# Sample outputs of attention, GLA and SSD: fold matmuls replaced by transposes, with copies or a DVE sum behind them

## The chip, the cores and the metric

The kernel runs on one core of a Trainium2 chip. The metric is the device time of one execution in microseconds. Three runs of the kernel before gave 2531.6, 2530.73 and 2526.93 us, the median is 2530.73 us.

A core has a matrix engine (TensorE, PE in the profile; its weight loads are PEld), a vector engine (DVE), a scalar engine (ACT) and GpSimd (POOL), which work through queues of their own, in order, and wait for one another through semaphores. SyncE (SP) issues transfers, POOL does too. Data lie in SBUF (128 partitions); TensorE writes PSUM, which DVE and ACT read.

## The reference, cut to what matters

One step of a decoder layer for two groups of tokens with the same weights: a prompt of 256 tokens, and 8 samples of 4 tokens (32 columns). All of it is float32.

```
xn = _rmsnorm(x, p['norm_mix'])
z, xbc, dt_raw, q, k, v, r, g_lr, gate_a, gate_b = _split(xn @ p['w_in'], IN_SIZES)
...
y_ssd, ssd_state_new = _ssd_scan(xs_h, dt, A, Bm, Cm, ssd_state)       # 32 heads in 4 groups
y_ssd = y_ssd + p['ssd_D'][:, None] * xs_h
u = y_ssd * silu(z);  u = u * rsqrt(mean(u * u) + EPS) * p['ssd_norm']
branch_a = u @ p['w_ssd_out']
...
o, gla_state_new = _gla_scan(qh, kh, vh, glog, gla_state)              # 4 heads
o = o * rsqrt(mean(o * o) + EPS) * p['gla_norm'] * silu(r)
branch_b = o @ p['w_gla_out']
merged = sigmoid(gate_a) * branch_a + sigmoid(gate_b) * branch_b
h = x + merged @ p['w_mix_out']
h = h + _cross_attend(_rmsnorm(h, p['norm_cross']), mem_k, mem_v, p['w_cq'], p['w_co'])   # 4 heads
up = _rmsnorm(h, p['norm_ffn']) @ p['w_up'];  ...  h = h + (silu(gt) * a) @ p['w_down']
```

For a sample, the part of a scan's output that matters here is a product with the sample's own state or memory: in SSD `einsum('bign,bgrpn->bigrp', Cc, S)`, in GLA `einsum('bihk,bhkv->bihv', qe, S)`, in attention `einsum('bhlm,bmhd->blhd', pr, mem_v)`. To it SSD and GLA add the part from the four tokens of the same sample.

## The kernel before

**Layout.** Activations lie with channels on the partitions and the T = 288 tokens in the columns: columns 0 to 255 are the prompt, 256 to 287 the samples (SEQ = 256, NS = 32, NB = 8 samples of NL = 4 tokens). A projection (`proj_w`, L132) goes over blocks of 256 output channels. For each pair of weight tiles ACT casts the raw tile to a high part (L103) and DVE subtracts it for a low part (L105); TensorE then does three matmuls for each weight tile (L147, L148 high part with both parts of the activations, L151 low part). Raw weights have 3 buffers, high and low parts 5 each. SP issues the weight transfers (L114).

**Stages.** Memory keys and values (L315 to L319); then eight units, the four SSD groups and the four GLA heads. `weave` (L172) runs the scan of unit n as background between the projection steps of unit n + 1 and the output projection of unit n - 1: the first 16 steps are of unit n + 1, and then `project(n - 1)` runs. After the last unit, `project(7)` follows at once. Then gates, mix, four cross-attention heads (`attend`, woven between query projections; the last head is woven between the first steps of the output projection `wo`), and the feed-forward part. The program gives the order in which the work is written; a scheduler with a timeline of its own decides each engine's order from it, except for instructions held with `keep_in_program_order` and a stretch at the start.

**The sample outputs.** The states of the 8 samples differ, so each sample needs a product of its own. With b = 4q + j (q 0 or 1, j 0 to 3), the product of sample b is written to the 32 partitions from 32j: the stationary operand (`qdm`, `cdm`, `pms`) holds 32 columns of which only 4b to 4b + 3 are not zero (`diag`, L191). Row 32j + 4b + l of the PSUM tile (L1138, L864, L1526) so holds the output of sample b, token l, and the other rows of the block only take zeros. In block j lie the samples j and 4 + j.

The part inside the four tokens is added in two ways. In GLA one matmul over all samples (L1133) with the mask tile `atsl` (filled at L1073 by `stack_l`: ACT's L655 for all 128 partitions, DVE's L656 for the last 64) puts it into rows 0 to 31. In SSD the heads are in two sets and L866 writes one set into rows 0 to 31 and the other into rows 32 to 63, each with all 32 sample tokens; DVE adds both to `ys` (L905, L908).

Then the 128 x 512 tile (`ys`, `os_`) is turned to channels on partitions, and its four blocks of rows are added: four matmuls with the 128 x 128 slice as stationary and `fold4` as moving operand, a 128 x 32 matrix of four identity matrices on top of each other (L914, L1161, L1554). Their outputs go side by side into a PSUM tile of tag `mm` (3 buffers).

**What follows each.** SSD: `us` (the D term) plus the result (L915), times silu(z) (L916), squares (L922, L925) added up by DVE (L926), then `finish`: L937 adds the squares over partitions by a matmul with ones, ACT makes the scale (L219, L220), DVE multiplies (L942) and splits into high and low part (L184, L185), tile `un`. GLA: `evac` squares on ACT (L1042) and multiplies on DVE (L1043), adds squares (L1044, L1045), then the same `finish`. Attention: `split` writes high (ACT, L188) and low (DVE, L189) part into `co`, the operand of the output projection.

`conv_cache` (L598) turns the state of the convolution, copies it with ACT (L603) to a tile of tag `cst` (2 buffers), and SP sends it out (L608). POOL issues the loads of the states: L727 and L715 in SSD, L1036 in GLA.

Of the kernel before, what the change touches and what calls it, by code (L numbers as in the profile page):

```python
# [8 lines left out]
F32 = mybir.dt.float32  # L9
# [3 lines left out]
ALU = mybir.AluOpType  # L13
AX = mybir.AxisListType
PSUM = bass.MemoryType.PSUM

P = 128
D = 2048
KT = D // P
SEQ = 256  # L20
NB = 8
NL = 4
NS = NB * NL
T = SEQ + NS
# [18 lines left out]
def hybrid_step(ctx: ExitStack, tc: tile.TileContext, I: dict, O: list):  # L43
# [3 lines left out]
    V, S, G = nc.vector, nc.scalar, nc.gpsimd  # L47
    MM, TR = nc.tensor.matmul, nc.tensor.transpose
# [12 lines left out]
    def acc_tiles(n):  # L61

        turn[0] += 1
        return [ps.tile([P, 512], F32, tag=f"acc{turn[0] % 2}", bufs=2, name="acc") for _ in range(n)]

    def mm_tile():
        return ps.tile([P, 512], F32, tag="mm", bufs=3, name="mm")
# [5 lines left out]
    ident = const.tile([P, P], F32, name="ident")  # L73
# [6 lines left out]
    fold4 = const.tile([P, NS], F32, name="fold4")  # L80
# [106 lines left out]
    def split(hi, lo, src):  # L187
        S.copy(hi, src)  # L188
        V.tensor_tensor(lo, src, hi, ALU.subtract)  # L189
# [13 lines left out]
    def halves(alloc, name):  # L203

        ts = [alloc(f"{name}{i}") for i in range(2)]

        def at(k, n=None):
            t, o = ts[k // 8], k % 8
            if n is None:
                return t[:, o, :], t[:, 8 + o, :]  # L210
            return t[:, o:o + n, :], t[:, 8 + o:8 + o + n, :]
        return at
# [40 lines left out]
    ats = p1.tile([P, NS], F32, name="ats")  # L253
    atsl = p1.tile([P, P], F32R, name="atsl")
# [11 lines left out]
    with pool("p0") as p0:  # L266
# [194 lines left out]
        for c in range(4):  # L461
            q = slice(c * NS, (c + 1) * NS)
# [112 lines left out]
    pa = pa_cm.__enter__()  # L575
# [4 lines left out]
    def b2(name):  # L580
        return pa.tile([P, 512], F32, tag="b2", bufs=10, name=name)
# [64 lines left out]
    def stack_r(dst, src):  # L646

        S.copy(dst, src)
        for q in (1, 3):
            rows = slice(q * NS, (q + 1) * NS)  # L650
            V.tensor_tensor(dst[rows], src[rows], dst[rows], ALU.subtract)

    def stack_l(dst, src):

        S.copy(dst, src)  # L655
        V.tensor_tensor(dst[2 * NS:], src[2 * NS:], dst[2 * NS:], ALU.subtract)  # L656
# [36 lines left out]
    def ssd_scan(g, xsT, sz):  # L693
# [39 lines left out]
        a = mm_tile()  # L733
# [9 lines left out]
        a = mm_tile()  # L743
# [9 lines left out]
        for i in range(2):  # L753
            a = mm_tile()
# [14 lines left out]
        a = mm_tile()  # L769
# [4 lines left out]
        a = mm_tile()  # L774
# [11 lines left out]
        for u in range(3):  # L786
# [19 lines left out]
            if prev is not None:  # L806
                uu, pm, pea = prev
                a = mm_tile()
                for w in range(2):
                    o = w * SEQ  # L810
                    for s in range(3):
                        for e in range(2):
                            q = 2 * w + e
                            hs = slice((4 * uu + q) * 64, (4 * uu + q + 1) * 64)
                            rows = slice(64 * e, 64 * e + 64)
# [27 lines left out]
        a = mm_tile()  # L843
# [6 lines left out]
        yield  # L850
        wst = r2("wst")
        stack_l(wst, wxs)
        yield

# [15 lines left out]
        for q in range(NB // 2):  # L870
# [12 lines left out]
            for t2 in range(2):  # L883
# [3 lines left out]
                a = mm_tile()  # L887
# [16 lines left out]
        ys = b2("ys")  # L904
        V.tensor_tensor(heads(ys), heads(ysi[0]), hb(eas[:, h0:h0 + 8], P), ALU.mult)  # L905
        for r in range(2):
            q, c = slice(NS * r, NS * r + NS), slice(256 * r, 256 * r + 256)
            V.tensor_tensor(ys[q, c], ys[q, c], ysa[0][q, c], ALU.add)  # L908
        us = b2("us").rearrange("p (t l) -> p t l", l=P)[:, :, 0:NS]
        V.tensor_tensor(us, xsT[:, :, SEQ:T], dcol[:, 4 * g:4 * g + 4].unsqueeze(2).to_broadcast([P, 4, NS]), ALU.mult)  # L910
        yield
        a = mm_tile()
        for t in range(4):
            MM(a[:, t * NS:(t + 1) * NS], ys[:, t * P:(t + 1) * P], fold4, start=True, stop=True)  # L914
        V.tensor_tensor(us, us, a[:, 0:4 * NS].rearrange("p (t l) -> p t l", l=NS), ALU.add)  # L915
        V.tensor_tensor(sz[:, :, SEQ:T], us, sz[:, :, SEQ:T], ALU.mult)  # L916
        yield

# [110 lines left out]
    def gla_scan(h, eb, qe, ke, kd, kde, vT, sr):  # L1029
# [9 lines left out]
        def evac(a, t0, n):  # L1039
            av = a[:, 0:4 * n].rearrange("p (t l) -> p t l", l=n)  # L1040
            s4 = b2("s4").rearrange("p (t l) -> p t l", l=P)[:, :, 0:n]
            S.activation(s4, av, ACT.Square)  # L1042
            V.tensor_tensor(sr[:, :, t0:t0 + n], av, sr[:, :, t0:t0 + n], ALU.mult)  # L1043
            V.tensor_tensor(s4[:, 0:2], s4[:, 0:2], s4[:, 2:4], ALU.add)  # L1044
            V.tensor_tensor(sq[:, t0:t0 + n], s4[:, 0, :], s4[:, 1, :], ALU.add)  # L1045
# [6 lines left out]
        for i in range(2):  # L1052
            a = mm_tile()
# [7 lines left out]
        a = mm_tile()  # L1061
        for i, (t0, n) in enumerate(TOK):
            for k in range(2):
                MM(a[:, t0:t0 + n], ke[:, k, t0:t0 + n] if i < 2 else ker[:, k, :], qe[:, k, t0:t0 + n],
                   start=(k == 0), stop=(k == 1))
        for i in range(2):
            for k in range(2):
                MM(a[:, 288 + 64 * i:352 + 64 * i], kd[:, k, P * i:P * i + P], qe[:, k, P * i + 64:P * i + P],
                   start=(k == 0), stop=(k == 1))
        V.copy_predicated(att, gmask.unsqueeze(1).to_broadcast([P, 2, P]),  # L1070
                          a[:, 0:SEQ].rearrange("p (c n) -> p c n", n=P))
        V.copy_predicated(ats, smaski, a[:, SEQ:T])
        stack_l(atsl[:, 0:NS], ats)  # L1073
        S.copy(att[0:64, :, 64:P], a[0:64, 288:416].rearrange("p (c n) -> p c n", n=64))
        for i in range(2):
            for k in range(2):
# [4 lines left out]
        a = mm_tile()  # L1081
# [5 lines left out]
        a = mm_tile()  # L1087
# [5 lines left out]
        a = mm_tile()  # L1093
        for k in range(2):
            TR(a[:, k * P:(k + 1) * P], ksr[:, k, :], ident)
        kst = pa.tile([P, 256], F32R, tag="kst", bufs=1, name="kst")
        stack_l(kst, a[:, 0:256])
        for k in range(2):
            diag(qdm[:, k], qe[:, k, SEQ:T])
# [7 lines left out]
        for i in range(2):  # L1107
            sn = c4([P, 2, 512], "sn")
            for k in range(2):
                a = mm_tile()  # L1110
# [7 lines left out]
            for t in range(4):  # L1118
                MM(o[:, t * P:(t + 1) * P], vt[i][:, t * P:(t + 1) * P], att[:, i, :], start=True, stop=(i == 0))
                if i == 1:  # L1120
                    for k in range(2):
                        MM(o[:, t * P:(t + 1) * P], sprev[:, k, t * P:(t + 1) * P], qe[:, k, P:SEQ], start=False,
                           stop=(k == 1))
# [10 lines left out]
        for q in range(2):  # L1134
            for k in (1, 0):
                for j in (3, 2, 1, 0):
                    b = 4 * q + j
                    MM(osa[NS * j:NS * j + NS, :], qdm[:, k, b, :], sins[b][:, k, :], start=False,  # L1138
                       stop=(q == 1 and k == 0))
            yield  # L1140
            for b in range(4 * q, 4 * q + 4):
# [3 lines left out]
                for k in range(2):  # L1145
                    a = mm_tile()
# [9 lines left out]
        os_ = b2("os")  # L1156
        S.copy(os_, osa)
        yield
        a = mm_tile()
        for t in range(4):  # L1160
            MM(a[:, t * NS:(t + 1) * NS], os_[:, t * P:(t + 1) * P], fold4, start=True, stop=True)  # L1161
        evac(a, SEQ, NS)
        yield
        yield
        yield from finish(sr, sq, rg, False)
# [69 lines left out]
    for n in range(8):  # L1235
        kind, i = units[n]
        scan = (ssd_scan if kind == "s" else gla_scan)(i, *outs[n][0])
        nxt = start(n + 1) if n < 7 else gate(O_GA, gate_a, GH)
        if n == 5:
            mb = bigf("mb")  # L1240
        parts = [nxt, gate(O_GA, gate_early, 0, GH)] if n == 0 else [steps(nxt, 16), project(n - 1), nxt]
        weave(chain(*parts), scan, N_MAIN[n], N_BG[n])
# [120 lines left out]
    co = halves(bigr2, "co")  # L1363
# [49 lines left out]
    def transpose_half(kv, d2):  # L1413

        a = mm_tile()
        for d in range(2):
            for m in range(2):
                dd = 2 * d2 + d
                TR(a[:, d * 256 + m * P:d * 256 + (m + 1) * P], kv[:, m, dd * P:(dd + 1) * P], ident)
        return a.rearrange("p (d m) -> p d m", m=256)  # L1420
# [30 lines left out]
    def attend(hd):  # L1451
# [26 lines left out]
        for d2 in range(2):  # L1478
            a = transpose_half(kvp[:, 0], d2)
# [4 lines left out]
        for l in range(2):  # L1484
            a = mm_tile()
# [18 lines left out]
        a = mm_tile()  # L1504
        TR(a[:, 0:P], pr, ident)
        for m in range(2):
            f, g = pms[:, m].rearrange("p b t -> p (b t)"), a[:, m * 64:(m + 1) * 64]
# [3 lines left out]
        a = mm_tile()  # L1511
# [11 lines left out]
        for q in (1, 0):  # L1523
            for m in range(2):
                for j in (3, 2, 1, 0):
                    mm = MM(osa[NS * j:NS * j + NS, :], pms[:, m, 4 * q + j, :], vcs[4 * q + j][:, m, :],  # L1526
                            start=(q == 1 and m == 0), stop=(q == 0 and m == 1))
# [9 lines left out]
        for d in range(4):  # L1537
            a = mm_tile()
# [10 lines left out]
        os_ = px.tile([P, 512], F32, tag="os", bufs=1, name="os")  # L1549
        S.copy(os_, osa)  # L1550
        yield
        a = mm_tile()
        for d in range(4):
            MM(a[:, d * NS:(d + 1) * NS], os_[:, d * P:(d + 1) * P], fold4, start=True, stop=True)  # L1554
        split(*(x[:, :, SEQ:T] for x in co(4 * hd, 4)),
              a[:, 0:4 * NS].rearrange("p (d l) -> p d l", l=NS))
        yield

    def first_keys():
# [11 lines left out]
    for hd in range(4):  # L1571
        main = q_proj(hd + 1) if hd < 3 else chain(steps(wo[0], 6), steps(wo[1], 6))
        weave(main, attend(hd), 16 if hd < 3 else 12, 22 if hd else 18)
# [158 lines left out]
    rows = [(0, slice(0, P)), (P, slice(0, P)), (T - P, slice(P - NS, P))]  # L1732
# [19 lines left out]
    a = acc_tiles(1)[0]  # L1752
# [62 lines left out]
```

## Time and profile before

| what | value |
|---|---|
| median of three runs | 2530.73 us |
| the profiled execution, own time | 2530.86 us |
| its span, first to last instruction | 2529.1 us |
| granted TensorE clock, mean | 0.997 |
| raw weight tiles cast by ACT (L103), mean | 618 ns, 1464 of them |
| their low parts on DVE (L105), mean | 686 ns, 1464 of them |
| fold matmul records (L914, L1161, L1554) | 96, mean 265 ns |
| traffic to and from HBM | 205 GB/s over the span |

How to read it: the profile names each group by line, engine, operation, output and inputs. A matmul's duration runs from its start to its modelled end, so successive matmuls overlap and their durations add to more than the time they take. The starts in the timeline show the pace. "Idle before" names the engine whose work the instruction waited for. The chain that ended last goes back from the last instruction, each time to what released it.

### The profile page before, as it was taken

The numbers are of one execution on the slowest core, as the hardware profiler recorded it, in microseconds if no ns is written. First come the engines' busy times: TensorE is split into PE (matmuls) and PEld (weight loads), VectorE is DVE, ScalarE is ACT, GpSimd is POOL, SyncE is SP. The second block draws the span as 40 slices with busy tenths as digits, with TensorE's granted clock in tenths as the row PEclk, the third lists the DMA queues.
The fourth block names the chain that finished last, engine by engine and source line by source line (L and its number), as shares of the span: only waits on it lengthen the run. The fifth ranks groups of instructions, "written<-read, shape, count | busy, mean of one in ns | idle before, by whom it ended". The sixth has DMA issues, their size and how long they took to land.

```text
span 2529.1 us, 50509 instructions
## 1 busy us (share of the span) xinstructions
PE 2508.4 (99%) x18962; PEld 2418.5 (96%) x18962; DVE 1747.9 (69%) x3744; ACT 1342.7 (53%) x2724; POOL 392.2 (16%) x729
## 2 busy tenths in 40 slices
PE   9999999999999999999999999999999999999998
PEld 8889999998999999999999998999999999999998
DVE  6656777786867656667666577667777677675765
ACT  7655647655463645454454554555555455454545
POOL 3002133342300000000001022402111001020010
PEclk9999999999999999999999999999999999999999
DMA  8766587767868676767777699655555555555553
GB/s 268 220 218 196 169 252 206 229 197 209 236 188 271 184 241 185 242 202 265 205 223 249 199 327 322 211 164 173 169 173 170 170 172 172 167 172 171 169 170 130
DMA packets 442022, 521.96 MB, mean 206 GB/s; under 512 B 26876, under 2 KB 390236, under 8 KB 441712
## 3 DMA queue, kind: packets, MB, share of 16 engines
q1 hardware_dynamic: 407728, 422.34, 54.3%
q0 software_dynamic: 34016, 96.38, 12.0%
q8 instruction: 149, 2.44, 0.4%
q14 instruction: 97, 0.79, 0.1%
q10 hardware_dynamic: 32, 0.01, 0.0%
HBM read 473.13 MB, written 45.48 MB: 205 GB/s over the span
## 4 chain that ended last, share of the span: by engine, by line
PE 96%; DMA 2%; DVE 1%; POOL 1%; ACT 0%; issue 0%; DVEq 0%; ACTq 0%
PE acc L148 27%; PE acc L147 27%; PE acc L151 27%; PE acc L315 2%; PE acc L316 2%; PE acc L319 2%; DMA sqr<-in_state_ssd_dram 1%; PE la L1526 1%; PE la L1468 1%; PE mm L1147 1%; PE la L1138 1%; PE mm L1111 1%; POOL sqr L727 0%; DMA raw<-in_w_gla_out_dram 0%; DMA raw<-in_w_in_dram 0%
## 5 line engine op out<-in xcount | busy, mean ns | idle before, releaser
L103 ACT CAST whi<-raw 128x512 fp32r<-128x512 f32 x1464 | 895.1, 618 | 1016.0 <-PE acc L148 753.2
L105 DVE TENSOR_TENSOR wlo<-raw,whi 128x512 fp32r<-128x512 f32 x1464 | 994.4, 686 | 621.5 <-ACT whi L103 607.9
L147 PE MATMUL acc<-xn,whi 128*128 128x288 f32 (+1 forms) x1936 | 550.5, 299 | 0.0
L148 PE MATMUL acc<-xn,whi 128*128 128x288 f32 (+1 forms) x1936 | 542.3, 296 | 0.0
L151 PE MATMUL acc<-xn,wlo 128*128 128x288 f32 (+1 forms) x1936 | 414.1, 295 | 0.0
L148 PE MATMUL acc<-hf,whi 128*128 128x288 f32 x1408 | 393.2, 295 | 0.0
L147 PE MATMUL acc<-hf,whi 128*128 128x288 f32 x1408 | 389.0, 292 | 0.0
L147 PEld LDWEIGHTS acc<-xn,whi 128*128 128x128 f32 (+1 forms) x1936 | 364.7, 188 | 9.8 <-issue 8.1
L148 PEld LDWEIGHTS acc<-xn,whi 128*128 128x128 f32 (+1 forms) x1936 | 365.0, 189 | 6.8 <-issue 4.9
L151 PEld LDWEIGHTS acc<-xn,wlo 128*128 128x128 f32 (+1 forms) x1936 | 310.5, 188 | 1.3 <-issue 1.1
L151 PE MATMUL acc<-hf,wlo 128*128 128x288 f32 x1408 | 294.5, 290 | 0.0
L148 PEld LDWEIGHTS acc<-hf,whi 128*128 128x128 f32 x1408 | 264.5, 188 | 0.1
L147 PEld LDWEIGHTS acc<-hf,whi 128*128 128x128 f32 x1408 | 264.0, 188 | 0.1
L151 PEld LDWEIGHTS acc<-hf,wlo 128*128 128x128 f32 x1408 | 226.1, 188 | 0.0
L148 PE MATMUL acc<-pr,whi 128*128 128x288 f32 x704 | 196.5, 295 | 0.0
L147 PE MATMUL acc<-pr,whi 128*128 128x288 f32 x704 | 195.0, 293 | 0.0
L147 PE MATMUL acc<-un,whi 128*128 128x288 f32 x512 | 145.8, 300 | 2.2 <-ACT whi L103 1.1
L151 PE MATMUL acc<-pr,wlo 128*128 128x288 f32 x704 | 147.4, 290 | 0.0
L148 PE MATMUL acc<-un,whi 128*128 128x288 f32 x512 | 142.9, 295 | 0.0
L1639 POOL COPY fsp<-fst 128x16 f32<-128x16 f32 x88 | 36.6, 419 | 656.5 <-DVE av L1651 422.0
L148 PEld LDWEIGHTS acc<-pr,whi 128*128 128x128 f32 x704 | 132.3, 188 | 0.0
L147 PEld LDWEIGHTS acc<-pr,whi 128*128 128x128 f32 x704 | 132.0, 188 | 0.0
(512 smaller groups left out, 4286.4 us busy)
## 6 DMA issues: line engine op xcount, KB each, us to landing
raw<-in_w_in_dram SPq DMA_DIRECT2D x240, 512.0 KB
raw<-in_w_up_dram SPq DMA_DIRECT2D x176, 512.0 KB
raw<-in_w_down_dram SPq DMA_DIRECT2D x88, 512.0 KB
raw<-in_w_cv_dram SPq DMA_DIRECT2D x32, 512.0 KB
raw<-in_w_ssd_out_dram SPq DMA_DIRECT2D x32, 512.0 KB
sin<-in_state_gla_dram POOLq DMA_DIRECT2D x32, 512.0 KB, 5.8
out_dram<-sin SPq DMA_DIRECT2D x32, 512.0 KB
raw<-in_w_gla_out_dram SPq DMA_DIRECT2D x32, 512.0 KB
```

The lines of the kernel that those rows point to most:

```text
L103: S.copy(hi, raw)
L105: V.tensor_tensor(lo, raw, hi, ALU.subtract)
L147: MM(a, hi[:, k, cs], xh, start=(k0 + s0 + k == 0), stop=False)
L148: MM(a, hi[:, k, cs], xl, start=False, stop=False)
L151: MM(a, lo[:, k, cs], xh, start=False, stop=(k0 + s0 + k == nk - 1))
L315: MM(accs[m], mn_hi[:, kk, ms_], hi[:, 0, :], start=(kk == 0), stop=False)
L316: MM(accs[m], mn_lo[:, kk, ms_], hi[:, 0, :], start=False, stop=False)
L319: MM(accs[m], mn_hi[:, kk, ms_], lo[:, 0, :], start=False, stop=(kk == KT - 1))
L1111: MM(a, kt[:, i, k * P:(k + 1) * P], vt[i], start=True, stop=True)
L1138: MM(osa[NS * j:NS * j + NS, :], qdm[:, k, b, :], sins[b][:, k, :], start=False, stop=(q == 1 and k == 0))
L1147: MM(a, kb[:, k * P:(k + 1) * P], vst, start=True, stop=True)
L1639: G.tensor_copy(sp[:, :, 0:2], st.rearrange("p (b k) -> p b k", k=2))
```

## The change

The twelve groups of four fold matmuls (4 SSD, 4 GLA, 4 attention) become four transposes each. A transpose gives 128 columns in place of 32, one for each row of the tile.

- Attention and GLA: the columns 36j + 16q + l are picked, for which `own` builds the address pattern. In attention `split` is called once for q = 0 and once for q = 1. In GLA two ACT copies bring the columns together in a new SBUF tile `ot` of tag `cst`, and `evac` reads that.
- GLA also writes the mask `atsl` so that the part inside the samples comes out in the rows 36j + 16q + l: the copy on ACT and the subtraction on DVE have a pattern of 2 x 4 x 4 columns in place of 32 in a row.
- SSD: DVE sums the four blocks with a `tensor_reduce` over a strided view of the PSUM tile, into a new tile `yt` of tag `cst`, and adds that to `us`.

```
+    def own(a, q):
+        return bass.AP(a.tensor, a.offset + 16 * q, [list(a.ap[0]), [P, 4], [NS + NL, 4], [1, NL]])
...
 # ssd_scan
-            MM(a[:, t * NS:(t + 1) * NS], ys[:, t * P:(t + 1) * P], fold4, start=True, stop=True)
-        V.tensor_tensor(us, us, a[:, 0:4 * NS].rearrange("p (t l) -> p t l", l=NS), ALU.add)
+            TR(a[:, t * P:(t + 1) * P], ys[:, t * P:(t + 1) * P], ident)
+        yt = pa.tile([P, P], F32, tag="cst", bufs=2, name="yt").rearrange("p (t l) -> p t l", l=NS)
+        V.tensor_reduce(yt, a.rearrange("p (t j l) -> p t l j", j=4, l=NS), axis=AX.X, op=ALU.add)
+        V.tensor_tensor(us, us, yt, ALU.add)
...
 # gla_scan
-        stack_l(atsl[:, 0:NS], ats)
+        for rows, op in ((slice(0, P), None), (slice(2 * NS, P), ALU.subtract)):
+            f, g = atsl[rows], ats[rows].rearrange("p (q j l) -> p q j l", j=4, l=NL)
+            f = bass.AP(f.tensor, f.offset, [list(f.ap[0]), [16, 2], [NS + NL, 4], [1, NL]])
+            if op is None:
+                S.copy(f, g)
+            else:
+                V.tensor_tensor(f, g, f, op)
...
-            MM(a[:, t * NS:(t + 1) * NS], os_[:, t * P:(t + 1) * P], fold4, start=True, stop=True)
-        evac(a, SEQ, NS)
+            TR(a[:, t * P:(t + 1) * P], os_[:, t * P:(t + 1) * P], ident)
+        ot = pa.tile([P, P], F32, tag="cst", bufs=2, name="ot")
+        for q in range(2):
+            S.copy(ot.rearrange("p (t q j l) -> p q t j l", t=4, q=2, j=4)[:, q], own(a, q))
+        evac(ot, SEQ, NS)
...
 # attend
-            MM(a[:, d * NS:(d + 1) * NS], os_[:, d * P:(d + 1) * P], fold4, start=True, stop=True)
-        split(*(x[:, :, SEQ:T] for x in co(4 * hd, 4)),
-              a[:, 0:4 * NS].rearrange("p (d l) -> p d l", l=NS))
+            TR(a[:, d * P:(d + 1) * P], os_[:, d * P:(d + 1) * P], ident)
+        for q in range(2):
+            split(*(x[:, :, SEQ + 16 * q:SEQ + 16 * q + 16].rearrange("p d (j l) -> p d j l", l=NL) for x in co(4 * hd, 4)),
+                  own(a, q))
```

## The prediction

> **What bounds the kernel now.** I read the page first: busy times, then the chain that ended last.
>
> ```profile
> span 2529.1 us, 50509 instructions
> ...
> PE 2508.4 (99%) x18962; PEld 2418.5 (96%) x18962; DVE 1747.9 (69%) x3744; ACT 1342.7 (53%) x2724; POOL 392.2 (16%) x729
> ...
> PE 96%; DMA 2%; DVE 1%; POOL 1%; ACT 0%; issue 0%; DVEq 0%; ACTq 0%
> ```
>
> TensorE carries 96% of the chain, and its weight loads are busy for nearly as long as its matmuls. So TensorE time that is taken out should shorten the run one for one, except where TensorE then waits. DVE (69%) and ACT (53%) have room on average, which says nothing of single places. Where TensorE waits today the view of waits tells:
>
> ```profile
> PE mm L890 <- ACT cst L603: 5.5, 1, 5.5
> ...
> PE acc L147 <- ACT whi L103: 1.1, 1, 1.1
> ...
> PE mm L777 <- DVE wx L761: 0.5, 1, 0.5
> PE acc L147 <- ACT co L188: 0.4, 1, 0.4
> ```
>
> These are the waits of places that the change can reach, each a single one, 7.5 us together (5.5 + 1.1 + 0.5 + 0.4). The long one is not ACT's doing. The chain in order of time, read around that place, shows a weight tile that took 8.9 us to land after state tiles had been loading:
>
> ```profile
> 552.48 5.39 DMA sqr<-in_state_ssd_dram
> ...
> 559.04 4.31 DMA sqr<-in_state_ssd_dram
> ...
> 565.21 8.90 DMA raw<-in_w_in_dram
> ...
> 574.73 0.61 ACT whi L103
> 575.35 0.17 ACT cst L603
> ```
>
> ACT's copy L603 stood in its queue behind the cast of that weight tile, and L890 behind the copy. I come back to it among the rivals.
>
> **TensorE: 12 groups of four.** Each SSD head group, GLA head and attention head ends in four fold matmuls; each becomes four transposes. The view of groups by shape has both kinds, since the kernel transposes elsewhere:
>
> ```profile
> L1554 PE MATMUL mm<-fold,os 128*128 128x32 f32 x32 | 3.9, 265 | 0.0
> L914 PE MATMUL mm<-fold,ys 128*128 128x32 f32 x32 | 3.9, 265 | 0.0
> L1161 PE MATMUL mm<-fold,os 128*128 128x32 f32 x32 | 3.9, 265 | 0.0
> ...
> L845 PE MATMUL mm<-ident,xsr 128*128 128x128 f32 x16 | 2.4, 272 | 0.0
> ```
>
> L1161 stands in a loop of four in four heads, 16 calls, and has 32 records: a fold is done in two passes. L845 is also a loop of four in four groups, and has 16 records: a transpose is one pass. So eight passes become four. Durations overlap (265 ns each), so the price is taken from starts, in the timeline around one group of each kind:
>
> ```profile
> 375.21 0.97 PE L914 MATMUL mm<-fold,ys 128*128 128x32 f32 x8
> ...
> 376.01 0.38 PE L147 MATMUL acc<-xn,whi 128*128 128x288 f32 x1
> ...
> 544.20 0.60 PE L845 MATMUL mm<-ident,xsr 128*128 128x128 f32 x4
> ...
> 544.55 0.38 PE L147 MATMUL acc<-un,whi 128*128 128x288 f32 x1
> ```
>
> From the first fold to the next projection matmul 0.80 us pass (376.01 - 375.21), from the first transpose 0.35 (544.55 - 544.20). The saving is 0.45 us a group, though the output is four times as wide: the pass counts, not its 32 or 128 columns. Eleven groups give 4.95 us.
>
> [...]
>
> **The twelfth group** is the last attention head's. Nothing else stands between it and the output projection:
>
> ```profile
> 1602.90 0.97 PE L1554 MATMUL mm<-fold,os 128*128 128x32 f32 x8
> 1603.10 0.37 ACT L188 CAST co<-mm 128x256 fp32r<-128x256 f32 x1 [0.22 <-PE mm L1543]
> 1603.52 0.42 DVE L189 TENSOR_TENSOR co<-mm,co 128x256 fp32r<-128x256 f32 x1
> 1603.91 0.27 ACT L188 CAST co<-mm 128x128 fp32r<-128x128 f32 x1 [0.44 <-PE mm L1554]
> 1604.21 0.29 DVE L189 TENSOR_TENSOR co<-mm,co 128x128 fp32r<-128x128 f32 x1 [0.27 <-ACT co L188]
> 1604.23 0.79 PE L147 MATMUL acc<-co,whi 128*128 128x288 f32 x4 [0.35 <-ACT co L188]
> ```
>
> The transposes end at 1602.90 + 0.60 = 1603.50, when ACT has just finished its copy before (1603.47). Then come two casts of 128x64 instead of one of 128x128. No row has that shape on ACT from PSUM; the nearest are 192 ns for 128x32 and 269 for 128x128:
>
> ```profile
> L620 ACT COPY cv<-acc 128x32 f32<-128x32 f32 x24 | 4.6, 192 | 0.0
> ...
> L1042 ACT ACTIVATE s<-mm 128x128 f32<-128x128 f32 x4 | 1.1, 269 | 0.1
> ```
>
> I take 0.23, the middle. Both end about 1603.54 + 2 x 0.23 = 1604.00, or 1603.92 to 1604.08 at the two ends, against 1604.18 now. So TensorE restarts 0.18 us earlier (0.10 to 0.26) instead of 0.45. DVE's two low parts follow while the four L147 run (0.79 us), so they hold nothing. Sum over twelve: 4.95 + 0.18 = 5.1 us.
>
> **What DVE and ACT get.** In SSD one add from PSUM is replaced by a reduction over all 512 columns and an add of 128. The nearest reductions and the third SSD group's finish:
>
> ```profile
> L1385 DVE TENSOR_REDUCE mx<-mm 128x1 f32<-128x256 f32 x8 | 3.4, 425 | 3.7 <-PE mm L1491 3.6
> ...
> L1402 DVE TENSOR_REDUCE mx<-la 128x1 f32<-128x128 f32 x4 | 1.2, 290 | 6.5 <-PE la L1468 6.5
> ...
> 614.50 0.97 PE L914 MATMUL mm<-fold,ys 128*128 128x32 f32 x8
> ...
> 615.51 0.29 DVE L915 TENSOR_TENSOR us<-us,mm 128x128 f32<-128x128 f32 x1 [1.31 <-PE mm L914]
> 616.32 0.28 DVE L916 TENSOR_TENSOR sz<-us,sz 128x128 f32<-128x128 f32 x1
> ...
> 617.45 1.59 DVE L926 TENSOR_TENSOR sqa<-sqa,th 128x288 f32<-128x288 f32 x3 [0.85 <-ACT th L925]
> ...
> 620.13 0.41 PE L937 MATMUL mm<-sqa,ones 128*128 128x288 f32 x1
> ```
>
> From 128 to 256 columns a reduction grows by 0.135 us, so 512 come to 0.425 + 2 x 0.135 = 0.70. Bounds: 0.43, the 256-column row, and 1.40, twice the line, since the four addends lie 32 columns apart and no row shows such a reduction. With L915 (0.29) as the price of the add, the path to the scale grows by 0.70 + 0.29 - 0.29 = 0.70. This group is the tightest: its L937 keeps its place in TensorE's order, while in the other three it stands 8, 9 and 32 matmuls later. DVE's last sum ends at 617.45 + 1.59 = 619.04, so L937 has 1.09 us of slack; DVE starts 0.45 earlier and so does TensorE, which leaves 1.09 - 0.70 = 0.39. A weight's low part (L105) now stands between L916 and L926, and the idle 0.85 before L926 takes it. At 1.40 the slack is gone by 0.31 us: TensorE would wait so long in this group, and behind it the projections. I count nothing, with 0.3 as its upper end.
>
> In GLA two ACT copies come ahead of L1042. Only the last head is followed at once by its consumer:
>
> ```profile
> 1180.18 0.65 PE L937 MATMUL mm<-sqa,ones 128*128 128x288 f32 x2
> ...
> 1186.13 1.80 DVE L185 SCALAR_TENSOR_TENSOR un<-sr,rg,un 128x288 fp32r<-128x288 f32 x4
> ...
> 1189.35 0.29 PE L147 MATMUL acc<-un,whi 128*128 128x288 f32 x1
> ```
>
> The normalized output is done at 1187.93, used at 1189.35: 1.42 us of cover. The change puts L937 four projection matmuls later, 0.13 each (0.53), and brings the use forward by 0.45; 0.44 is left. Were the cover gone, each tenth would be paid in full. The two copies (0.46) lie within the 0.53. The mask's moved pieces hold as many elements as before, and their one reader, L1133, comes only after both chunk steps of the head. SP and POOL keep their order, so no DMA is added or moved past another. The new tile shares two buffers with the convolution-state staging, whose transfers are few and far apart:
>
> ```profile
> L608 SPq DMA_DIRECT2D out_dram<-cst x16: 734/797/886, 232.8 to 576.3; - x16
> ```
>
> Sixteen in 343 us, under 1 us each to issue: by the time that a buffer comes round, two uses later, its transfer should long have landed. Were it not so, DVE's reduction would wait and with it all L105 behind it. No charge.
>
> The profiled run was 2530.86 us, span 2529.1 and 1.8 around it; the median of the runs is 2530.73. Less 5.1 that is 2525.8 and 2525.6. I take 2525.6. This kernel's measurement tells about 0.2% (5.06 us) from no change, so the forecast stands right on that bound.
>
> **The rivals.**
> 1. *Savings swallowed by transfers.* If the weight tiles in the third and fourth SSD groups come at a time that state loads set and not TensorE, the 1.8 us saved by four groups ahead of or in that stretch are waited away: 2530.7 - 3.3 = 2527.4. For it: the 8.90 us landing. Against it: the state buffers are freed by DVE work that follows TensorE, so the whole pattern should shift along.
> 2. *The transfer wait dissolves.* A shift of 0.9 us lets the weight tile go ahead of one state load; the 5.5 us wait goes too: 2525.6 - 5.5 = 2520.1. For it: the three runs spread from 2526.93 to 2531.6, so something of that size comes and goes.
> 3. *It repeats* (the other side): the same collision, weight tile behind state loads, strikes two more of the SSD groups, each at 5.5 us: 2525.6 + 11 = 2536.6. One more is not enough (2531.1); it decides once the added waits exceed 5.1 + 5.06 us. Against it: SP's and POOL's order is unchanged, and only one group of four suffers now.
> 4. *Transposes in sequence*, 272 ns each: 4 x 0.27 = 1.09 us a group against 0.80, 12 x 0.29 = 3.5 us lost: 2534.2. It is also the case in which the change does not do what it says. Against it: four took 0.35 us above.
>
> **How the numbers follow.** Forecast 0.55, within 1.5 us either way; as it stands on the bound, and as rival 2 in part would pull below it, I give 0.40 to faster by over 0.2% and 0.15 to within. Rival 1: 0.16, within. Rival 2: 0.15, faster. Rival 3: 0.09, slower. Rival 4: 0.02, within. Another slower cause that I do not see: 0.03. So faster 0.55, within 0.2% 0.33, slower 0.12. The range goes from 2520.0, rival 2's middle, to 2531.5, past rival 1 and no change; outside it lie half of rival 2, rivals 3 and 4 and the unseen cause, 0.2; the likeliest case alone is 2524.1 to 2527.1.
>
> **What would show it.** 16 records each of the new transposes at about 272 ns; 0.35 us from the first to the next projection matmul; the reduction near 0.70 us; TensorE still without a wait at L937; the wait before L147 at the output projection about 0.3 us longer; L890's wait still near 5.5. TensorE's busy sum should fall by about 5 us with DVE's up by about 3. The prediction is wrong if the transposes follow at more than 0.2 us each, if L937 or the next head's projections wait for DVE, or if the state loads' waits change by more than the 5 us that are saved.

## The result, and the profile after

| | before | after |
|---|---|---|
| median | 2530.55 us (5 runs, 2526.93 to 2531.6) | 2519.75 us (5 runs, 2516.66 to 2522.44) |
| profiled execution, own time | 2530.86 us | 2522.44 us |

The ratio is 0.9969, 95% interval 0.9957 to 0.998: faster by 0.31%. The forecast was 2525.6 us (0.20%), so the direction came out as forecast and the gain is twice as large: 10.8 us between the medians, 8.4 between the two profiled executions, against 5.1.

The page of the kernel after, its span, busy times and chain:

```profile
span 2520.7 us, 50431 instructions
...
PE 2502.4 (99%) x18914; PEld 2411.9 (96%) x18914; DVE 1753.1 (70%) x3752; ACT 1346.9 (53%) x2736; POOL 392.8 (16%) x729
...
PE 95%; DMA 2%; DVE 1%; ACT 1%; issue 0%; POOL 0%; DVEq 0%; ACTq 0%; POOLq 0%
```

TensorE is busy for 6.0 us less (2508.4 before) and still carries 95% of the chain. The view of single lines has the new operations of the kernel after, with their shortest, median and longest duration in ns:

```profile
L918 PE MATMUL mm<-ident,ys x16: 270/272/273, 374.3 to 703.6; 128*128 128x128 f32 x16
...
L920 DVE TENSOR_REDUCE yt<-mm x4: 683/684/692, 375.5 to 706.3; 128x128 f32<-128x512 f32 x4
...
L921 DVE TENSOR_TENSOR us<-us,yt x4: 283/288/291, 376.2 to 707.9; 128x128 f32<-128x128 f32 x4
...
L1176 ACT COPY ot<-mm x8: 198/208/226, 832.3 to 1169.5; 128x64 f32<-128x64 f32 x8
```

There are 16 records of the transposes where the fold had 32 (the same for L1173 in GLA and L1569 in attention). The timeline around the first SSD group, where the fold took 0.80 us to the next projection matmul:

```profile
374.30 0.60 PE L918 MATMUL mm<-ident,ys 128*128 128x128 f32 x4
374.65 0.38 PE L147 MATMUL acc<-xn,whi 128*128 128x288 f32 x1
```

It takes 0.35 now. The waits of TensorE in the kernel after, each total, count and longest:

```profile
PE mm L894 <- ACT cst L603: 3.4, 1, 3.4
...
PE acc L147 <- ACT co L188: 0.9, 1, 0.9
PE acc L147 <- DVE mb L961: 0.8, 1, 0.8
PE la L1483 <- DVE xqm L1462: 0.4, 1, 0.4
```

L894 is L890 of before. Its wait is shorter by 2.1 us, the one at the output projection is longer by 0.5, one at L1483 is new, and L943 (L937 before) has none. In the GLA output projection the wait of 1.1 us for the cast L103 is gone; the one of 0.8 us for DVE's sum L961 now stands there.

Where the 8.4 us of the two profiled executions lie follows from the starts of the twelve groups and of the stages between them. Eleven groups give 0.45 each and the twelfth loses 0.13: 4.8. The third SSD group gives 2.8 beside its passes. The stretch ahead of the first scan, in which nothing is changed, gives 0.9. The output projection of GLA gives 0.6 beside its passes. The rest sums to -0.7, in attention above all. So the passes are near the forecast, and 3.4 us came from two places with waits, the third SSD group (2.8) and the output projection of GLA (0.6). Which of these belong to the change, and which to the single execution, is what the experiments ask.

### The profile page after: what moved, and what is told of

Same layout as the page of the kernel before. It is cut to its first block, busy times and chain, and to the rows that moved or that the text cites. A ratio compares the mean times of both kernels' runs of the same rounds, so it can differ in the third digit from the quotient of the medians.

```text
span 2520.7 us, 50431 instructions
## 1 busy us (share of the span) xinstructions
PE 2502.4 (99%) x18914; PEld 2411.9 (96%) x18914; DVE 1753.1 (70%) x3752; ACT 1346.9 (53%) x2736; POOL 392.8 (16%) x729
## 4 chain that ended last, share of the span: by engine, by line
PE 95%; DMA 2%; DVE 1%; ACT 1%; issue 0%; POOL 0%; DVEq 0%; ACTq 0%; POOLq 0%
PE acc L148 27%; PE acc L147 27%; PE acc L151 26%; PE acc L315 2%; PE acc L316 2%; PE acc L319 2%; PE la L1541 1%; PE mm L1159 1%; PE la L1150 1%; DMA sqr<-in_state_ssd_dram 1%; PE la L1483 1%; PE mm L1123 1%; DMA sin<-in_state_ssd_dram 1%; DMA raw<-in_w_gla_out_dram 0%; POOL sqr L731 0%
## 5 line engine op out<-in xcount | busy, mean ns | idle before, releaser
L103 ACT CAST whi<-raw 128x512 fp32r<-128x512 f32 x1464 | 897.3, 618 | 1011.9 <-PE acc L148 783.6
L105 DVE TENSOR_TENSOR wlo<-raw,whi 128x512 fp32r<-128x512 f32 x1464 | 997.2, 687 | 607.9 <-ACT whi L103 590.5
```

Of the source, the lines that this page charges most:

```text
L103: S.copy(hi, raw)
L105: V.tensor_tensor(lo, raw, hi, ALU.subtract)
```

## The experiments

"Difference" below is the mean time of a kernel minus that of the kernel before in the same series on the same chip, with its standard error.

### The kernel before, once more

The same program, as a measure of the scatter.

> The kernel before, unchanged. Shows how far the medians of five runs and the wait before L890 differ between two sets of the same kernel. Theory A: median within 1.5 us of the kernel before, wait before L890 between 5 and 6 us. Theory B: the wait itself comes and goes, so that it may be 3.5 us or less here.

Median 2528.36 us against 2527.76, ratio 1.0007 (0.9995 to 1.0019): no difference, but single executions of before in that series reach from 2521.31 to 2539.32. The profiles show where. This view has TensorE's busy time with its count of matmuls, then weight loads, DVE, ACT, POOL, the granted clock, the DMA share and GB/s. Before, in two stretches of 8 us around the wait before L890:

```profile
568.00:576.00 8.00, 2.51 (x18) 2.24 (x18) 4.43 (x11) 1.30 (x4) 4.89 (x8) 0.87 1.07 312
576.00:584.00 8.00, 8.00 (x46) 8.00 (x46) 5.45 (x14) 2.48 (x4) 0.00 (x0) 0.70 0.88 258
```

And the same program again, the same two stretches:

```profile
568.00:576.00 8.00, 6.40 (x49) 6.12 (x48) 5.37 (x12) 2.33 (x5) 5.08 (x8) 1.00 1.08 320
576.00:584.00 8.00, 8.00 (x62) 7.43 (x61) 6.10 (x15) 2.98 (x8) 0.71 (x1) 1.00 1.04 324
```

47 matmuls more fit into the 16 us (111 against 64), 6.1 us at 0.13 each. The wait that the prediction took as a fixed 5.5 us is 1.6 here, and the clock stays at 1.00, where in the other execution it was granted at half for 6.8 us, the last 5.2 of them behind the wait. The DMA share around the wait is 1.07 and 1.08. The weight tile ahead of the wait took 8.9 us to land in the first of these executions, 6.8 in the kernel after, whose wait is 3.4, and 5.1 in the kernel with the GLA part alone, whose wait is 1.7; so the same transfer takes another time in each of these profiles. A second place, the gate and mix projections, again first the one and then the other execution of before:

```profile
1215.00:1400.00 185.00, 185.00 (x1407) 185.00 (x1406) 116.54 (x214) 89.47 (x170) 15.94 (x27) 1.00 0.74 228
```

```profile
1215.00:1400.00 185.00, 185.00 (x1378) 185.00 (x1377) 117.54 (x214) 90.64 (x171) 15.89 (x27) 1.00 0.72 225
```

TensorE is busy throughout at a granted clock of 1.00 and yet does 1378 matmuls in place of 1407: 134.3 against 131.5 ns each by the count (134.4 and 131.7 by the starts). From the first matmul of the feed-forward part to the end, on the other hand, every profile of this study takes 842.02 or 842.03 us. The scatter lies in the first 1690 us alone.

### One part alone

Each part of the change by itself, the other two left as before.

```
e1: only ssd_scan      +TR(a[:, t * P:(t + 1) * P], ys[...], ident) ... +V.tensor_reduce(yt, ...)
e2: only gla_scan      +TR(a[:, t * P:(t + 1) * P], os_[...], ident) ... +S.copy(ot..., own(a, q)), atsl
e3: only attend        +TR(a[:, d * P:(d + 1) * P], os_[...], ident) ... +split(..., own(a, q))
```

> SSD groups changed alone. Theory A (the surplus over the forecast came from the weight-tile wait before L890 in the third SSD group and the slow TensorE clock behind it, which the four SSD groups shift): time about 1.8 us of passes plus 3 to 6 us less than the kernel before, about 2524 to 2526, and a wait before L890 under 4 us. Theory B (each part gives its passes only, the rest is scatter from run to run): 1.8 us less, about 2528.7, wait before L890 near 5.5 us.

> GLA heads changed alone; nothing differs before 700 us. Theory A and theory B agree: 4 x 0.45 = 1.8 us less, about 2528.7, with the wait before L890 as in the kernel before (near 5.5 us). If it gains 4 us or more, both are wrong and the surplus lies in GLA.

> Attention heads changed alone. Three groups give 0.45 us each, the fourth loses about 0.1 us because the second copy to the high part waits for DVE: 1.2 us less, about 2529.3, by theory A and theory B. The wait before L147 at the output projection is 0.8 to 0.9 us instead of 0.4.

| | median, us | ratio (95%) | difference, us | four groups' passes |
|---|---|---|---|---|
| SSD | 2525.11 | 0.999 (0.998 to 1.0) | -1.7 ± 1.3 | -1.8 |
| GLA | 2524.44 | 0.9986 (0.9973 to 1.0) | -2.8 ± 1.2 | -1.8 |
| attention | 2525.1 | 0.9989 (0.998 to 0.9998) | -2.5 ± 1.1 | -1.2 |

Each part gains, and the three add up to -7.0 ± 2.6 (they share one set of runs of the kernel before). None is told from its passes alone by its time. The wait before L890 (L894) is 3.3, 1.7 and 1.6 us in the three profiles, and 1.6 in the kernel before of the same series: it goes with the execution, not with the edit. The 3.3 us of the SSD part lie where they were expected if the edit shortens the wait, but that tells nothing beside the 1.6 of the unchanged kernel; for the GLA part 5.5 had been expected.

### The kernel after, twice more

> The changed kernel, unchanged, in a dozen runs. Theory B, now split: the passes give 4.8 us (11 x 0.45 less 0.1), and the rest of the first comparison (5 runs each) was scatter, the wait before L890 (1.6 to 5.5 us in four runs of the kernel before) and the pace of the projections: the difference of the means comes to -4 to -6.5 us. Theory C (the new order of instructions really saves more): -8 us or more, as in the first comparison.

> The changed kernel once more, as the reference for the next run on the same chip. Theory (about 5 us from TensorE passes, 1.5 to 2 us from waits on raw weights, the rest of the first comparison scatter): 5 to 9 us below the kernel before, and between the first transpose of the last GLA head and the last matmul of the GLA output projection 38.3 to 40.1 us. Rival (the first comparison's 10.8 us is the true size): 10 to 12 us below.

The two series give medians of 2520.65 against 2528.39 (ratio 0.9973, 0.9956 to 0.9991) and 2519.76 against 2528.88 (0.9967, 0.9955 to 0.9979). The differences of the means are -5.9 ± 2.3 and -8.2 ± 1.2, the first comparison's is -9.7 ± 1.4; weighted together -8.4 ± 0.9. So the 10.8 us between the first medians are too many, and 5.1 too few: some 3 us more than the passes belong to the change.

### Every transpose done twice

```
-            TR(a[:, t * P:(t + 1) * P], ys[:, t * P:(t + 1) * P], ident)
+            for _ in range(2):
+                TR(a[:, t * P:(t + 1) * P], ys[:, t * P:(t + 1) * P], ident)
```

The same in GLA and attention: as many passes as the fold had, with the rest of the change kept.

> The changed kernel with each of the 48 transposes done twice into the same place. Theory B: 48 passes more at 0.11 us, 5.3 us above the changed kernel, so within 1.5 us of the kernel before; from the first new transpose to the next projection matmul 0.79 us. If transposes were dearer than their pace shows (each new pass waiting for the one before), it is 10 us or more above the changed kernel.

The timeline at the first SSD group:

```profile
374.81 1.04 PE L919 MATMUL mm<-ident,ys 128*128 128x128 f32 x8
375.60 0.38 PE L147 MATMUL acc<-xn,whi 128*128 128x288 f32 x1
```

Eight transposes take 0.79 us to the next projection matmul, as the eight passes of the fold did (0.80). The median is 2528.39 us, ratio to before 1.0003 (0.9992 to 1.0014); the mean is 6.7 ± 2.4 us above the kernel after in this series. With the passes given back the whole gain is gone within the error: the copies, the mask and the DVE sum gain nothing by themselves.

The run gives back more than the passes, however. ACT's queue in the last GLA head, whose transposes begin at 1171.13:

```profile
1175.15 0.62 ACT L103 CAST whi<-raw 128x512 fp32r<-128x512 f32 x1 [0.99 <-PE acc L148]
1175.79 1.28 ACT L219 ACT_TABLE_LOAD   x1
1177.08 0.50 ACT L219 ACTIVATE rstd<-mm,epsc 128x288 f32<-128x288 f32 x1
1177.48 0.61 ACT L103 CAST whi<-raw 128x512 fp32r<-128x512 f32 x1
```

This is the order of the kernel before, which the change alters (the section after the next), and in the second attention head too TensorE's order is that of before. So the 6.7 ± 2.4 us are the 48 passes (5.3 at 0.11 each) together with the two orders that went back with them; this run does not tell these apart.

### Without the state loads of the third SSD group

The square state loads of that group (L727, L731) are left out, a constant takes their place, in the kernel before and in the kernel after.

```
+            if g == 2:
+                G.memset(sq_, 0.5)
+            else:
                 for i in range(4):  # the four loads
```

> The kernel before with the square state loads of the third SSD group (L727, 8 tiles) left out: POOL fills those tiles with a constant, so the sample outputs of that group are not computed. If the wait before L890 comes from those loads it is below 0.5 us, the TensorE clock is never halved near 570 us, and the time falls by 2 to 6 us. If the wait has another cause (the row-wise state tiles, the weight loads alone) it stays above 1.5 us.

> The changed kernel with the same loads left out. Theory B: 4.8 us below the kernel before with them left out (3.5 to 6.5 with the scatter), since the passes are all that the change takes away. Theory C, as far as the wait in the third group carried the surplus: the same 4.8 us here, but 8 or more for the changed kernel with its loads.

The wait before L890 (L894), 5.5 and 3.4 us with the loads, is gone in both, so the loads are what makes it, and the clock is 1.00 from 570 to 585 us, with 115 and 114 matmuls. In its place the waits for DVE's sums of the output projections, which free the accumulators, are longer (L955 in the kernel before with its loads: 1.1 us). Without the loads, in the kernel before

```profile
PE acc L147 <- DVE ma L958: 3.3, 3, 1.5
```

and in the kernel after

```profile
PE acc L147 <- DVE ma L964: 5.0, 3, 3.1
```

The medians are 2526.67 and 2519.82 us, and the means differ by 6.5 ± 0.9. In the kernel before the loads' absence alone brings 1.6 ± 0.9 us, less than the 2 to 6 expected. The long wait is thus not what the change needs in order to gain: the gain is 6.5 without it and 8.4 ± 0.9 with it, a difference of 1.9 ± 1.2 that these runs do not resolve.

### The last GLA head

From the first fold or transpose of the last GLA head to the start of the last matmul of the GLA output projection the profiles with a fold there had shown 39.3 to 41.2 us, those with single transposes 38.3 to 39.4. 0.45 of that are the passes. The queue of ACT shows another difference. The kernel before, whose fold begins at 1175.33:

```profile
1177.74 0.62 ACT L103 CAST whi<-raw 128x512 fp32r<-128x512 f32 x1 [1.12 <-PE acc L148]
1179.32 0.62 ACT L103 CAST whi<-raw 128x512 fp32r<-128x512 f32 x1 [0.96 <-PE acc L148]
1179.96 1.28 ACT L219 ACT_TABLE_LOAD   x1
1181.25 0.50 ACT L219 ACTIVATE rstd<-mm,epsc 128x288 f32<-128x288 f32 x1
1181.65 0.61 ACT L103 CAST whi<-raw 128x512 fp32r<-128x512 f32 x1
```

The kernel after, whose transposes begin at 1168.65:

```profile
1170.59 0.62 ACT L103 CAST whi<-raw 128x512 fp32r<-128x512 f32 x1 [0.51 <-PE acc L148]
1172.15 0.62 ACT L103 CAST whi<-raw 128x512 fp32r<-128x512 f32 x1 [0.94 <-PE acc L148]
1173.71 0.62 ACT L103 CAST whi<-raw 128x512 fp32r<-128x512 f32 x1 [0.94 <-PE acc L148]
1174.35 1.28 ACT L219 ACT_TABLE_LOAD   x1
```

The third cast of a raw weight stood behind the table load and the scale; now it stands ahead of them. It comes 5.06 us after the group's start in place of 6.32. DVE's low part (L105) follows the cast and frees the raw buffer, and right behind it SP issues the next but one transfer, 6.61 us after the start in place of 7.68. Two kernels test this: the change in the last GLA head alone, and the fold kept, with ACT copies put between it and the squares, which make the scheduler take the new order.

```
e11, kernel before:    +if h == 3: transposes, own(), ot, atsl as in the change; else the fold
e12, kernel before:     fold4 kept, then if h == 3:
+            ot = ...; two S.copy(ot..., a...)        # all columns, q = 0 and q = 1
+            for _ in range(3): o2 = ...; S.copy(o2, ot); ot = o2
+            evac(ot, SEQ, NS)
```

> The kernel before with the change in the last GLA head alone. Theory (the last head moves ACT's third cast of a raw weight ahead of the scale, so the raw weights of the GLA output projection are asked for about 1 us earlier): from the head's first transpose to the last matmul of that projection 38.3 to 39.1 us, where runs with the fold there show 39.3 to 41.2; no wait for a weight's high or low part in it. Rival (the gain needs the earlier heads too, or is only the 0.45 us of passes): 40.0 to 40.3 us.

> The kernel before, fold kept, with five small ACT copies between the fold and the squares of the last GLA head: they change nothing that is computed, but make the scheduler put three casts of raw weights ahead of the scale there, as in the changed kernel. Theory (ACT's order counts, not the passes): the raw weights are asked for earlier and the stretch is shorter by 1 to 1.5 us, 38.7 to 39.5, unless TensorE then waits for the normalized output, which the waits would show as L147 behind un. Rival (the passes make it, or it is scatter): 40.3 to 41.2 as before.

The queue of ACT in the second one, whose fold begins at 1174.48:

```profile
1176.88 0.62 ACT L103 CAST whi<-raw 128x512 fp32r<-128x512 f32 x1
...
1178.46 0.62 ACT L103 CAST whi<-raw 128x512 fp32r<-128x512 f32 x1 [0.75 <-PE acc L148]
1180.04 0.62 ACT L103 CAST whi<-raw 128x512 fp32r<-128x512 f32 x1 [0.96 <-PE acc L148]
1180.68 1.28 ACT L219 ACT_TABLE_LOAD   x1
```

The new order with the fold kept: the third cast 5.56 us after the start, the transfer at 6.94. The whole list of profiles ("end" is the start of the last matmul):

| from the group's start, us | third cast | SP's transfer | end of the projection |
|---|---|---|---|
| fold, ACT's order as before: five profiles | 6.32 | 7.68 | 40.52, 40.50, 39.28, 41.22, 40.69 |
| fold, new order | 5.56 | 6.94 | 39.20 |
| transposes done twice, in all heads; ACT's order as before | 6.35 | 7.71 | 40.11 |
| transposes in the last head alone | 5.06 | 6.61 | 39.31 |
| transposes in all heads: six profiles | 5.06 | 6.61 | 38.30, 39.43, 38.30, 38.30, 38.42, 38.30 |

The casts and issues come out the same to 0.01 us in each profile of a row, so their place is set by the order of the queue. The end scatters, in the first row from 39.28 to 41.22. The mean is 40.44 in the first row and 38.62 in the last two, 1.8 ± 0.4 less. Of that 0.45 are passes.

Another 0.5 is pace. By their starts TensorE's projection matmuls follow at 130.0 ns just ahead of this group, in all fourteen profiles. Behind single transposes they go on at 130.0 (all seven profiles), behind a fold or doubled transposes at 131.7 to 131.8 (all seven), and some 290 of them come before the end of the projection.

That leaves 0.9 ± 0.4 us for the earlier transfer. It shows as waits of TensorE in the projection: 1.1 to 1.6 us in four of the five profiles of the first row and 0.6 with the transposes doubled, but 0.8 and 0.7 in only two of the eight profiles in ACT's new order. That the order alone does it, the second row makes likely (39.20, no wait in the stretch) but does not show: the one profile of the first row without a wait is as short (39.28). The last head alone came out at 39.31, 0.2 above what was expected of it, with one of these waits, 0.7 us for DVE's sum. The times of the two single runs are 2532.95 and 2527.97 us, within the spread of before (2522.08 to 2535.8 in that series).

### Both high parts ahead of the low parts

In attention the first half is cast and its low part subtracted before the second half is cast. Here both casts come first.

```
-        for q in range(2):
-            split(*(...), own(a, q))
+        for (hi, _), src in parts:
+            S.copy(hi, src)
+        for (hi, lo), src in parts:
+            V.tensor_tensor(lo, src, hi, ALU.subtract)
```

> The changed kernel with both high-part casts of an attention head ahead of both low parts. Theory (the second cast waits 0.34 us for DVE's first low part): in the last head the second cast follows the first without a wait, the first L147 of the output projection waits about 0.5 us instead of 0.86, and the time is about 0.3 us less than the changed kernel's, below what the timing can tell. Rival (the cast waits for something else, the PSUM tile or its queue): the wait of 0.86 us stays.

The timeline of the kernel after at the last attention head (of two L188 in a row, the second is the first 128x64 cast):

```profile
1594.42 0.60 PE L1569 MATMUL mm<-ident,os 128*128 128x128 f32 x4
1594.62 0.65 ACT L188 CAST co<-mm 128x256 fp32r<-128x256 f32 x2 [0.35 <-PE mm L1558]
1595.03 0.56 DVE L189 TENSOR_TENSOR co<-mm,co 128x256 fp32r<-128x256 f32 x2
...
1595.61 0.21 ACT L188 CAST co<-mm 128x64 fp32r<-128x64 f32 x1 [0.34 <-DVE co L189]
...
1595.88 0.79 PE L147 MATMUL acc<-co,whi 128*128 128x288 f32 x4 [0.86 <-ACT co L188]
```

And with the casts first:

```profile
1590.89 0.60 PE L1569 MATMUL mm<-ident,os 128*128 128x128 f32 x4
...
1591.53 0.33 ACT L1573 CAST co<-mm 128x64 fp32r<-128x64 f32 x2
...
1591.91 0.80 PE L147 MATMUL acc<-co,whi 128*128 128x288 f32 x4 [0.42 <-ACT co L1573]
```

In the kernel after ACT's second small cast waits 0.34 us for DVE's first low part, which itself stood behind the low part of the product before. With the casts first there is no such wait, the two take 0.33 us together, and from the first transpose to the output projection 1.02 us pass in place of 1.46 (before: 1.33). That is 0.44 us better at this place. The whole time shows nothing of it: 2520.74 us, ratio to before 0.9972 (0.9958 to 0.9986), mean 1.0 ± 1.5 above the kernel after of the same series.

## Why the prediction was right, and where its sizes were off

- **Passes.** Right. Four transposes follow at 0.11 us and 0.35 us pass to the next projection matmul, in all groups but the last and the third SSD group, where one projection matmul stands among the four (0.49 us for the five). Rival 4, transposes in sequence, is out: 272 ns is a duration, not a pace. The distances come back in every profile with single transposes, and the run with doubled ones agrees: its eight passes take 0.79 us.
- **The twelfth group.** Wrong in sign. The two casts have the predicted size (0.21 us against 0.23), but the step took it that they follow one another; the second waited for DVE. The term is -0.13 us where +0.18 (0.10 to 0.26) was counted, and with the casts first it is +0.31 (1.33 - 1.02).
- **The SSD sum.** 0.68 us against an estimate of 0.70, and no wait at L943. DVE's busy time rises by 5.2 us in place of 3; the four reductions are 2.7 of it.
- **Covers counted at nothing.** In the second attention head the product with the keys comes 2 us earlier in TensorE's order than in the kernel before, and its 128 matmuls take 3.96 us by their starts, not 3.63, in each of the six profiles with single transposes in attention (with the transposes doubled, order and 3.63 are as before). That loses 0.33 us and was not foreseen. Together with the twelfth group the sum of what the edits do by themselves is 4.95 - 0.13 - 0.33 = 4.5 us, not 5.1.
- **The output projection of GLA.** This is the mis-sized term. The prediction followed that head's scale and its use, found 0.44 us of cover left and charged nothing; it showed the wait of 1.1 us for a cast in that projection among those that the change can reach, and gave it no term. It kept ACT's queue as it was but for the copies, where the scheduler moved a weight cast of the next projection ahead of the scale. The profiles show about 1.4 us less there beside the passes: 0.9 in waits, and 0.5 by a faster pace of the matmuls, which the prediction took as fixed. 4.5 + 1.4 = 5.9.
- **The long wait, rivals 1 to 3.** The prediction expected 5.5 us to stay, with 0.15 for its going altogether. It is neither: in the six profiles without the SSD edit that keep the loads it is 5.5, 1.6, 1.7, 1.6, 4.9 and 6.2 us, in the six with it 3.4, 3.3, 3.1, 1.8, 2.8 and 2.4. Without the state loads it is gone, so it comes of them, and its length differs from one execution to the next. The clock at half behind it, another 2 us in the profile of before (18 matmuls in place of 32 in 4 us), had no price at all. Rival 3, the same collision in more groups, did not come.
- **What stays open.** 8.4 ± 0.9 less 5.9 leaves 2.5 ± 0.9 us. Two places can hold it. One is the third SSD group: from its predecessor's fold to its own the six profiles with the fold and the loads take 114.1, 114.1, 114.2, 119.9, 120.3 and 120.4 us, five with transposes 115.4 to 117.1. The mean is 1.0 lower, 0.45 of it passes, with an error of 1.4: not resolved. The other is the pace in the gate and mix projections, right behind the GLA output projection. They take 202.2 us in six of the seven profiles with a fold or doubled transposes in the last GLA head and 206.5 in the seventh. In the five profiles with the whole change and single transposes they take 202.2, 202.2, 200.6, 199.7 and 199.7, with the same matmuls and the clock at 1.00. That is 2.0 ± 0.8 less. The three short ones are those in which the pace of 130.0 ns behind the transposes outlasted the GLA output projection, and no wait is listed there. So the pace may well be most of what is left; but no run changes it alone, and what sets it was not found.

The prediction's own mechanism, the passes with what directly follows them, is thus worth 4.5 us. The other 3.9 of the 8.4 were not foreseen.

The forecast's range began at 2520.0 us, 0.25 above the median of the first comparison; the two later ones lie at 2520.65 and 2519.76.

## What to carry to other kernels

Price a small TensorE operation by the distance of starts and by its number of passes, not by its duration or its columns: here four 128-column transposes of one pass took 0.35 us to the next matmul, four 32-column float32 matmuls of two passes 0.80. After an edit ahead of a stage that reads weights, compare the order of the casts that free weight buffers, on the engine that makes them: here a cast that moved ahead of a normalization brought a transfer forward by 1.07 us (6.61 after the group's start in place of 7.68). Compare the distance of TensorE's starts behind the edit as well, where no wait is listed. And before a single long wait behind a transfer is made a term of the sum, profile the unchanged kernel twice; here the wait was 5.5 and 1.6 us in the two profiles of the kernel before, and anything from 1.6 to 6.2 in all that keep the loads.

## What the hardware showed that was not expected

**Half clock around a wait.** The same 4 us of the span, in the kernel with copies ahead of the last GLA head's squares (wait of 4.9 us before L890) and in the kernel after (3.4 us); the number ahead of the DMA share is the clock:

```profile
576.00:580.00 4.00, 4.00 (x18) 4.00 (x18) 2.49 (x9) 0.00 (x0) 0.00 (x0) 0.50 0.85 257
```

```profile
576.00:580.00 4.00, 4.00 (x32) 4.00 (x31) 1.74 (x6) 0.75 (x2) 0.00 (x0) 1.00 1.02 328
```

At a granted clock of 0.50 TensorE does 18 matmuls, at 1.00 it does 32. By stretches of 0.5 us the phase lasted 6.8 us in the kernel before, from 573.9 to 580.8, with the end of the wait at 575.56 inside it, and 3.4 in the kernel after, from 572.5 to 575.9, with the end of the wait at 571.67 ahead of it. The length of the wait does not decide it by itself: with a wait of 1.8 us (kernel after, third series) the mean clock from 572 to 576 us was 0.62, with one of 3.3 us (SSD part alone) it was 1.00. What decides it no run shows.

**Pace at full clock.** At the same granted clock of 1.00, with TensorE busy throughout, the matmuls of the gate and mix projections come at three paces. The kernel before did 1407 and 1378 in the 185 us above; the kernel with both casts first does 1425 of the same matmuls:

```profile
1215.00:1400.00 185.00, 185.00 (x1425) 185.00 (x1424) 122.13 (x224) 94.50 (x179) 16.42 (x28) 1.00 0.75 234
```

By their starts these are 131.7, 134.4 and 130.0 ns each. The pace goes with what came before: behind eight passes in the last GLA head it went from 130.0 to 131.7 in seven profiles of seven, behind four it stayed at 130.0 in seven of seven. It changed again at a wait in the GLA output projection in two profiles: from 131.7 to 134.4 at one of 1.6 us (the kernel before once more), from 130.0 to 131.7 at one of 0.8 us (the kernel after). In the third series of the kernel after it went from 130.0 to 131.7 there without a listed wait. No run shows what sets it.
